# Half-array fp32 products of a hybrid decoder's mixers, issued with the halves alternating

## The chip, the cores and the metric

The kernel runs on one core of a Trainium2 chip. The metric is the device time of one execution in microseconds (us).

## What is computed

One inference step of a decoder trunk with two layers, for a prompt of 512 tokens and eight sample sequences of eight tokens each; all are held as 576 token columns. A layer normalizes the residual, projects it with one matrix, runs four token mixers on parts of the result, adds their output projection, and then an MLP:

```python
h = rmsnorm(x, P['norm_mix_w'][li])
proj = jnp.einsum('bld,de->ble', h, P['w_in'][li]).astype(jnp.float32)
...
mix = jnp.concatenate([y_ssd, y_swa, y_hg, y_lru], axis=-1).astype(dtype)
x = x + jnp.einsum('ble,ed->bld', mix, P['w_out'][li])
h2 = rmsnorm(x, P['norm_mlp_w'][li])
up = jnp.einsum('bld,df->blf', h2, P['w_up'][li])
x = x + jnp.einsum('blf,fd->bld', jnp.square(jax.nn.relu(up)), P['w_down'][li])
```

Three of the mixers have products of 64-wide heads: HGRN2 (a gated linear recurrence), SSD (Mamba-2) and attention in a sliding window. The two recurrences work in chunks. A chunk's output is the sum of a term from inside the chunk and one from the state before it, as here for HGRN2:

```python
o_intra = jnp.einsum('bchts,bcshv->bcthv', A, v)
...
o_inter = jnp.einsum('bcthk,bchkv->bcthv', q * jnp.exp(bc), S_in)
o = (o_intra + o_inter).reshape(b, nc * T, H, V)[:, :L]
```

## The kernel before, in words

Features lie on the partitions, tokens in the columns. The large products (`product`, line 336; the MLP's seven-product form at line 1089) split each fp32 operand into two parts that the array takes at one pass each and add three products per block; their results are called pi (input projection), pd (output and down projection), pu and p. The mixers' own products are plain fp32, and each of them appears in the profile as two instructions.

A recording layer takes the program in the order of the code and a scheduler orders each engine's instructions from it; each engine then runs its own queue in order. The projections of the next mixer fill PE's queue between the steps of the mixer before it.

The products that the change touches have two heads, or two groups, one on partitions 0 to 63 and the other on 64 to 127, and use 64 rows or 64 columns of the array, or both:

- HGRN2, `hgrn`, once for each of two pairs of heads per layer. After the four products u (line 578), from which VectorE (DVE) makes the running states hst (line 585), o is written by products of 128 rows and 64 columns (line 595, the term inside a chunk; four chunks, two heads) and added to by products of 64 rows and 64 columns (line 597, the term from the state, chunks 1 to 3). For every chunk and head the adding product follows the writing one. Then the samples' os, one head after the other: one writing product (line 603) and eight adding ones of eight columns (line 605). The products us (line 612) follow. DVE reads o at line 598 and os at line 606.
- SSD, `ssd`, for each of two groups g per layer: four products G (line 718; 64 rows, 128 columns) at the head of the group's turn and one Gs for the samples, later y (lines 781 and 783) and ys (lines 788 and 791), built as o and os are, with both halves j of the output on the same 64 rows in the adding products. DVE reads y at line 784 and ys at line 792.
- Attention, `swa`: the samples' aos (lines 941 and 943), then four blocks of queries in staggered steps: the logits lg (line 962), one kv head i after the other, and the output ao (line 993), head by head, each over its blocks of keys.

```python
for i in range(2):
    r = slice(64 * i, 64 * i + 64)
    for e in range(2):
        for k in range(nk):
```

PSUM tiles of the mixers come from `bank`: five banks in turn; the large products have three of their own.

Of the kernel before, what the change touches and what calls it, by code (L numbers as in the profile page):

```python
# [14 lines left out]
ALU = mybir.AluOpType  # L15
AX = mybir.AxisListType
PSUM = bass.MemoryType.PSUM
# [13 lines left out]
CW = 600                 # columns of a causal convolution over the padded row  # L31
# [15 lines left out]
# columns of the packed per-layer vectors  # L47
# [9 lines left out]
# columns of the constants  # L57
# [7 lines left out]
# tiles of 128 columns of w_in, in the order of their use  # L65
# [48 lines left out]
class Pool:  # L114
    """A pool of tiles by role: t(tag) allocates the next tile of that role."""
# [15 lines left out]
def seqs(t, w=NT):  # L131
    """the sample columns as [rows, sequence, w]; w = 11 in padded rows"""
    o = NP_ if w == NT else NP_ + 3
    return t[:, o : o + NB * w].rearrange("p (b t) -> p b t", b=NB)


def staggered(parts):
    """run the parts' steps so that each part is one step behind the one before it"""
    n = 0
    while parts:  # L140
        n += 1
        for p in parts[:n]:
            if next(p, True):
                parts.remove(p)
                n -= 1


class Kern:
# [14 lines left out]
    # ---- small helpers  # L163
# [28 lines left out]
    # ---- constants and everything that is loaded once  # L192
# [75 lines left out]
            # sample rows (r, e, t) of 32-row groups: sequence b = 4 * u + r, head 2 * i + e  # L268
# [11 lines left out]
    def lower_bounds(self):  # L280
        """log of HGRN's lower bound of layer 1 and of its complement (layer 0's bound is zero by construction)."""
# [25 lines left out]
    # ---- weights: float32 = hi + lo, both exact in float32r; eight blocks of 128 x 128  # L307
# [18 lines left out]
    def product(self, name, blocks, put):  # L326
        """put(half, columns, sum over the blocks (wh, wl, xh, xl) of w.T @ x in that half of the columns);
        behind a norm the first products run ahead of 1/rms, which their put() needs"""
# [17 lines left out]

    def silu(self, out, in_):
        return self.nc.scalar.activation(out, in_, AF.Silu)

    def exp_ln(self, ins):  # L350
        """the tables of exp and ln again, behind the last use of others"""
# [3 lines left out]
    # ---- RMSNorm over the model dimension: split (x * w) for the products, 1/rms as a factor of their results  # L355
# [31 lines left out]
    def rstd(self, r, sqs, scale, ones):  # L387
        """r = (mean over features + eps)^-1/2, on every partition; ones adds the rows that belong together."""
# [8 lines left out]
    # ---- input projection of one tile of columns -> [128, T] in PSUM, times 1/rms into dst  # L397
# [38 lines left out]
    def history(self, xp, hist, out):  # L436
        """the padded row's history columns, and the last three columns of each sequence as the new history"""
# [14 lines left out]
    def to_tokens(self, src, dst):  # L452
        """[128 features, T] -> tokens on partitions, [128, 4 x 128 | 128], the last block with 64 rows"""
# [10 lines left out]
    def by_sequence(self, dst, src):  # L464
        """dst [64, b, n] = src [64 tokens, n] in the rows of sequence b, else 0"""
# [19 lines left out]
    def hgrn(self, p):  # L485
# [6 lines left out]
        # log sigmoid(f), log f, k  # L492
# [29 lines left out]
        # pairs (s, t) by the level at which their blocks meet; every exponent is <= 0  # L522
# [37 lines left out]
        # c is now the running sum within a chunk  # L560
# [11 lines left out]
        # states  # L572
# [16 lines left out]
        # o  # L589
        ps = self.bank("o")  # L590
        for ci in range(4):
            a = slice(128 * ci, 128 * ci + 128)
            for d in range(2):
                r = slice(64 * d, 64 * d + 64)
                nc.tensor.matmul(ps[r, a], vt[:, 128 * ci + 64 * d : 128 * ci + 64 * d + 64], A[:, d, a], start=True, stop=ci == 0)  # L595
                if ci:
                    nc.tensor.matmul(ps[r, a], sts[ci][r], q[r, a], start=False, stop=True)
        V.tensor_tensor(o[:, :NP_], ps, o[:, :NP_], op=ALU.add)
        # samples
        p2 = self.bank("os")  # L600
        for d in range(2):
            r = slice(64 * d, 64 * d + 64)
            nc.tensor.matmul(p2[r, :NS], vt[:, NP_ + 64 * d : NP_ + 64 * d + 64], A[:, d, NP_:T], start=True, stop=False)
            for b in range(NB):
                nc.tensor.matmul(p2[r, NT * b : NT * b + NT], S0[r, b], q[r, NP_ + NT * b : NP_ + NT * b + NT], start=False, stop=b == NB - 1)  # L605
# [10 lines left out]
        # the norm by head, the gate  # L616
# [8 lines left out]
    # ---- SSD  # L625
# [3 lines left out]
    def ssd_dt(self):  # L629
        """dt, the running sum of dt * A, and exp(last - sum): rows = heads"""  # L630
# [27 lines left out]
        # tokens on partitions: [128, chunk, (dt | sum | exp(last - sum)), head]  # L658
# [9 lines left out]
        # C's factor exp(sum) for the two heads of a group, and its last values  # L668
# [12 lines left out]
    def ssd(self):  # L681
# [28 lines left out]
        sqs = []  # L710
        for g in range(2):
            rg = slice(64 * g, 64 * g + 64)
            # decay[s, t] = exp(sum_t - sum_s) where t >= s, times B_s . C_t
            gm = P.t("b", SLOT, bufs=2)
            ps = self.bank("G")
            for ci in range(4):
                a = slice(128 * ci, 128 * ci + 128)
                nc.tensor.matmul(ps[:, a], B[rg, a], C[rg, a], start=True, stop=True)
# [12 lines left out]
            # exp(min(., 0))  # L731
# [5 lines left out]
            # tokens on partitions: x dt, x dt exp(last - sum)  # L737
# [16 lines left out]
            # the states before each chunk and after the last one  # L754
# [19 lines left out]
            # y  # L774
            y, dp = X[g], self.par("sD", g)
            ps = self.bank("y")
            for j in range(2):
                r = slice(64 * j, 64 * j + 64)
                for ci in range(4):
                    a = slice(128 * ci, 128 * ci + 128)  # L780
                    nc.tensor.matmul(ps[r, a], xs[:, 128 * ci + 64 * j : 128 * ci + 64 * j + 64], D[j][:, a], start=True, stop=ci == 0)  # L781
                    if ci:
                        nc.tensor.matmul(ps[r, a], new[ci - 1][rg, j], self.cs[j][rg, a], start=False, stop=True)
            V.scalar_tensor_tensor(y[:, :NP_], y[:, :NP_], dp, ps, op0=ALU.mult, op1=ALU.add)
            p2 = self.bank("ys")
            for j in range(2):
                r = slice(64 * j, 64 * j + 64)
                nc.tensor.matmul(p2[r, :NS], xs[:, NP_ + 64 * j : NP_ + 64 * j + 64], D[j][:, NP_:T], start=True, stop=False)
                for b in range(NB):
                    a = slice(NP_ + NT * b, NP_ + NT * b + NT)  # L790
                    nc.tensor.matmul(p2[r, NT * b : NT * b + NT], S0T[rg, b, j], self.cs[j][rg, a], start=False, stop=b == NB - 1)  # L791
# [15 lines left out]
    # ---- RG-LRU  # L807
    def lru(self, xps, gs):
# [4 lines left out]
        # -8 softplus(-lambda)  # L813
# [12 lines left out]
        for p, xp in enumerate(xps):  # L826
# [8 lines left out]
            V.tensor_scalar(r[:, p, :CW], r[:, p, :CW], lr[:, p : p + 1], None, op0=ALU.mult)      # log a  # L835
        # gelu's tanh
# [13 lines left out]
        # 1 - a^2 = tanh(-log a) (1 + a^2)  # L850
# [6 lines left out]
        # the column before a sample's first token carries its state  # L857
# [15 lines left out]
    # ---- sliding-window attention; q tile e holds heads (e, 2 + e) on the partitions of kv heads (0, 1)  # L873
    def swa(self, Q, K, Vv):
# [23 lines left out]
        # samples: rows (r, e, t) in groups of 32, blocks (i, u), sequence b = 4 * u + r  # L898
# [7 lines left out]
        Ls = [P.t("L", [2, 256], bufs=4) for _ in range(2)]      # by kv head  # L906
# [31 lines left out]
        p2 = self.bank("aos")                            # [128 (i d), u, r, 32]  # L938
        for i in range(2):
            r = slice(64 * i, 64 * i + 64)  # L940
            nc.tensor.matmul(p2[r, :256], vts[:, r], pn[:64, i], start=True, stop=False)
            for b in range(NB):
# [438 lines left out]
```

## Time and profile before

| | |
|---|---|
| median of three runs | 1412.06 us (1411.49 to 1412.78) |
| span of the profiled execution | 1412.2 us |
| time of the profiled execution beside its span | none is given apart from the span; the median of the runs is 0.1 us under it |
| PE (matmul) busy | 1388.7 us, 98% |
| DVE busy | 1031.7 us, 73% |
| ACT busy | 651.7 us, 46% |
| first layer: mixers and output projection | 0 to 322 us |
| second layer: the same | 705 to 1013 us |

The rest of the span is the MLPs, 383 and 399 us. PE's records overlap, since matmuls are pipelined: the distance from a group's start to the next group's start tells what it costs, the duration of a record does not. The clock column (PEclk) is the share of TensorE's full clock that was granted in a stretch.

### The profile page before, as it was taken

The page shows a single profiled execution, that of the slowest core. Times are in us where ns is not written, and L with a number is a line of the kernel's source. Part 1 is how long each engine was busy: PE and PEld are TensorE (multiplying, and loading weights), DVE is VectorE, ACT ScalarE, POOL GpSimd, SP SyncE. Part 2 cuts the span into 40 slices and gives each one's busy share as a digit, 9 for nine tenths or more (in the row PEclk, how much of TensorE's full clock was granted, in tenths as well). Part 3 has the DMA queues.
Part 4 walks back from the last instruction along what each step waited for, and adds up shares of the span by engine and source line. Part 5 has one row for each costly group of instructions (what it writes and reads, how often), then busy time and mean ns, then how long its engine had stood idle before and what let it go on. Part 6 is the DMA issues. An engine that isn't in the chain of part 4 may idle for free.

```text
span 1412.2 us, 25457 instructions
## 1 busy us (share of the span) xinstructions
PE 1388.7 (98%) x10376; PEld 1326.4 (94%) x10376; DVE 1031.7 (73%) x2059; ACT 651.7 (46%) x1167; POOL 64.6 (5%) x125
## 2 busy tenths in 40 slices
PE   7999999999999999999999999999999999999997
PEld 7898889899999999999998989898999999999997
DVE  7966687668777778777668768764886877778765
ACT  6455427566433344333453734456662433343334
POOL 4010101100000000000000000010000000000000
PEclk9999999999999999999999999999999999999999
DMA  7142323312232223232330323130232223223221
GB/s 252 47 145 101 103 72 103 99 58 89 79 103 93 88 76 105 75 104 85 125 128 27 118 77 107 66 136 31 83 113 75 76 91 105 80 72 105 90 75 67
DMA packets 39716, 131.33 MB, mean 93 GB/s; under 512 B 5960, under 2 KB 8128, under 8 KB 39568
## 3 DMA queue, kind: packets, MB, share of 16 engines
q1 hardware_dynamic: 29312, 102.12, 21.2%
q0 software_dynamic: 6544, 22.65, 4.7%
q10 hardware_dynamic: 3744, 4.95, 1.0%
q8 instruction: 81, 1.33, 0.4%
q14 instruction: 35, 0.29, 0.1%
HBM read 120.32 MB, written 11.34 MB: 93 GB/s over the span
## 4 chain that ended last, share of the span: by engine, by line
PE 90%; DVE 4%; ACT 3%; issue 1%; DMA 1%; DVEq 0%; ACTq 0%
PE pd L336 33%; PE p L1089 21%; PE pi L336 16%; PE pu L336 5%; PE sc L544 2%; PE pl L1241 2%; PE ss L393 1%; PE ao L993 1%; PE y L781 1%; PE pdt L336 1%; PE o L595 1%; DMA cs<-acd 1%; PE os L605 1%; ACT hi L323 1%; PE ys L791 1%
## 5 line engine op out<-in xcount | busy, mean ns | idle before, releaser
L336 PE MATMUL pd<-fh,hi 128*128 128x288 f32 x960 | 283.8, 296 | 0.0
L336 PE MATMUL pd<-fl,hi 128*128 128x288 f32 x960 | 283.7, 296 | 0.0
L336 PE MATMUL pd<-fh,lo 128*128 128x288 f32 x960 | 283.6, 295 | 0.0
L323 ACT CAST hi<-raw 128x1024 fp32r<-128x1024 f32 x134 | 140.3, 1047 | 287.2 <-PE pd L336 154.6
L336 PE MATMUL pi<-xh,hi 128*128 128x288 f32 x704 | 213.4, 304 | 7.4 <-ACT xh L368 7.4
L336 PE MATMUL pi<-xl,hi 128*128 128x288 f32 x704 | 214.0, 304 | 0.7 <-DVE xl L369 0.7
L336 PE MATMUL pi<-xh,lo 128*128 128x288 f32 x704 | 213.9, 304 | 0.0
L323 DVE TENSOR_TENSOR lo<-raw,hi 128x1024 fp32r<-128x1024 f32 x134 | 163.6, 1221 | 24.3 <-ACT hi L323 23.4
L336 PEld LDWEIGHTS pd<-fh,hi 128*128 128x128 f32 x960 | 181.1, 189 | 0.0
L336 PEld LDWEIGHTS pd<-fl,hi 128*128 128x128 f32 x960 | 181.0, 189 | 0.0
L336 PEld LDWEIGHTS pd<-fh,lo 128*128 128x128 f32 x960 | 180.6, 188 | 0.0
L1024 DVE TENSOR_TENSOR x<-x,pd 128x288 f32<-128x288 f32 x240 | 107.9, 450 | 99.5 <-PE pd L336 99.3
L336 PEld LDWEIGHTS pi<-xh,hi 128*128 128x128 f32 x704 | 136.1, 194 | 11.7 <-ACT xh L368 7.4
L336 PEld LDWEIGHTS pi<-xh,lo 128*128 128x128 f32 x704 | 136.2, 193 | 4.2 <-issue 3.2
L336 PEld LDWEIGHTS pi<-xl,hi 128*128 128x128 f32 x704 | 135.9, 193 | 2.9 <-DVE xl L369 1.2
L1089 PE MATMUL p<-Th,ul 128*128 128x288 f32 x312 | 92.0, 295 | 0.0
L1089 PE MATMUL p<-Th,uh 128*128 128x288 f32 x312 | 92.0, 295 | 0.0
L1089 PE MATMUL p<-Tl,uh 128*128 128x288 f32 x312 | 92.0, 295 | 0.0
L1089 PE MATMUL p<-xh,ul 128*128 128x288 f32 x312 | 91.9, 295 | 0.0
L1089 PE MATMUL p<-xl,uh 128*128 128x288 f32 x312 | 91.7, 294 | 0.0
L1089 PE MATMUL p<-xh,uh 128*128 128x288 f32 x312 | 91.7, 294 | 0.0
L1065 ACT CAST uh<-raw 128x1024 fp32r<-128x1024 f32 x52 | 54.5, 1048 | 66.8 <-PE p L1089 44.1
(487 smaller groups left out, 3114.1 us busy)
## 6 DMA issues: line engine op xcount, KB each, us to landing
raw<-in_wu SPq DMA_DIRECT2D x64, 512.0 KB, 3.2
raw<-in_wd SPq DMA_DIRECT2D x64, 512.0 KB, 4.3
raw<-in_wi SPq DMA_DIRECT2D x44, 512.0 KB, 3.3
raw<-in_wo SPq DMA_DIRECT2D x16, 512.0 KB, 3.2
x<-in_xT SPq DMA_DIRECT2D x8, 288.0 KB, 5.5
a<-acd ACTq DMA_DIRECT2D x4, 576.0 KB, 3.9
xl<-in_xT POOLq DMA_DIRECT2D x8, 288.0 KB, 4.2
xd<-x POOLq DMA_DIRECT2D x8, 288.0 KB, 2.4
```

The lines of the kernel that those rows point to most:

```text
L323: self.split_ins = nc.scalar.copy(hi, raw).ins, nc.vector.tensor_tensor(lo, raw, hi.bitcast(F32), op=ALU.subtract).ins
L336: self.nc.tensor.matmul(out, w, x[:, a], start=n == 0, stop=n == last)
L393: nc.tensor.matmul(ps[:, :TH], ones, s[:, TH * h : TH * h + TH], start=n == 0, stop=n == len(sqs) - 1)
L544: nc.tensor.matmul(pv[:, :, 64 * ci : 64 * ci + 64], kE[:, 128 * ci : 128 * ci + 128], qE[:, :, 64 * ci : 64 * ci + 64], start=True, stop= ...
L595: nc.tensor.matmul(ps[r, a], vt[:, 128 * ci + 64 * d : 128 * ci + 64 * d + 64], A[:, d, a], start=True, stop=ci == 0)
L605: nc.tensor.matmul(p2[r, NT * b : NT * b + NT], S0[r, b], q[r, NP_ + NT * b : NP_ + NT * b + NT], start=False, stop=b == NB - 1)
L781: nc.tensor.matmul(ps[r, a], xs[:, 128 * ci + 64 * j : 128 * ci + 64 * j + 64], D[j][:, a], start=True, stop=ci == 0)
L791: nc.tensor.matmul(p2[r, NT * b : NT * b + NT], S0T[rg, b, j], self.cs[j][rg, a], start=False, stop=b == NB - 1)
L1024: self.nc.vector.tensor_tensor(y[:, a], x[:, a], ps, op=ALU.add)
L1065: S.copy(hl[0], src)
L1089: nc.tensor.matmul(ps[:, :TH], u, x, start=j == 0, stop=j == 11)
L1241: nc.tensor.matmul(ps, u[:, o + q], v[:, a], start=j == 0, stop=j == 11)
```

## The change

A helper `tiled` issues a list of products; o and os, y and ys, aos and ao are now lists in which all writing products come first and the adding ones behind them, with the two halves of the partitions taking turns in both. Only the first two products of a list are marked as starting an accumulation and only the last two as ending it. In SSD the G products of both groups are issued together ahead of the groups, alternating, into two banks. In attention both lg tiles of a block are made ahead, and their products alternate between the kv heads. Comments go too. The instructions of every engine are the same ones before and after; only their order differs.

```diff
+    def tiled(self, products):
+        for n, (out, w, x) in enumerate(products):
+            self.nc.tensor.matmul(out, w, x, start=n < 2, stop=n >= len(products) - 2, skip_group_check=True)
...
         ps = self.bank("o")
-        for ci in range(4):
-            a = slice(128 * ci, 128 * ci + 128)
-            for d in range(2):
-                r = slice(64 * d, 64 * d + 64)
-                nc.tensor.matmul(ps[r, a], vt[:, 128 * ci + 64 * d : 128 * ci + 64 * d + 64], A[:, d, a], start=True, stop=ci == 0)
-                if ci:
-                    nc.tensor.matmul(ps[r, a], sts[ci][r], q[r, a], start=False, stop=True)
+        self.tiled([(ps[64 * d : 64 * d + 64, 128 * ci : 128 * ci + 128], vt[:, 128 * ci + 64 * d : 128 * ci + 64 * d + 64],
+                     A[:, d, 128 * ci : 128 * ci + 128]) for ci in range(4) for d in range(2)]
+                   + [(ps[64 * d : 64 * d + 64, 128 * ci : 128 * ci + 128], sts[ci][64 * d : 64 * d + 64],
+                       q[64 * d : 64 * d + 64, 128 * ci : 128 * ci + 128]) for ci in range(1, 4) for d in range(2)])
...
+        self.tiled([(p2[half(d), :NS], vt[:, NP_ + 64 * d : NP_ + 64 * d + 64], A[:, d, NP_:T]) for d in range(2)]
+                   + [(p2[half(d), NT * b : NT * b + NT], S0[half(d), b], q[half(d), NP_ + NT * b : NP_ + NT * b + NT])
+                      for b in range(NB) for d in range(2)])
...
+        G = [self.bank("G") for g in range(2)]
+        for ci in range(4):
+            a = slice(128 * ci, 128 * ci + 128)
+            for g in range(2):
+                nc.tensor.matmul(G[g][:, a], B[64 * g : 64 * g + 64, a], C[64 * g : 64 * g + 64, a], start=True, stop=True)
         for g in range(2):
...
-            ps = self.bank("G")
-            for ci in range(4):
-                a = slice(128 * ci, 128 * ci + 128)
-                nc.tensor.matmul(ps[:, a], B[rg, a], C[rg, a], start=True, stop=True)
+            ps = G[g]
...
+            lg = [self.bank("lg").rearrange("p (e n) -> p e n", e=2) for i in range(2)]
+            for e in range(2):
+                for i in range(2):
+                    nc.tensor.matmul(lg[i][:, e, :n], Q[e][kv(i), a], K[kv(i), s0 : s0 + n], start=True, stop=True)
...
-            for i in range(2):
-                r = slice(64 * i, 64 * i + 64)
-                for e in range(2):
-                    for k in range(nk):
-                        kb = s0 // 128 + k
-                        nc.tensor.matmul(po[r, e], vt[:, 128 * kb + 64 * i : 128 * kb + 64 * i + 64],
-                                         PT[i][:, e, 128 * k : 128 * k + 128], start=k == 0, stop=k == nk - 1)
+            at = lambda i, k: s0 + 128 * k + 64 * i
+            self.tiled([(po[kv(i), e], vt[:, at(i, k) : at(i, k) + 64], PT[i][:, e, 128 * k : 128 * k + 128])
+                        for k in range(nk) for e in range(2) for i in range(2)])
```

The lists of y and ys and of aos are made in the same way.

Where the instructions stand. On PE, in the first HGRN2 pair of layer 0, behind the products u, the later part of o and os stood so before (a row is one program instruction, two in the profile; xN counts equal ones in a row; the numbers tell tiles apart):

```order
L595 MATMUL o_623<-A_157,vt_448 64x128
L597 MATMUL o_623<-q_307,hst_609 64x128
L595 MATMUL o_623<-A_157,vt_448 64x128
L597 MATMUL o_623<-q_307,hst_609 64x128
L595 MATMUL o_623<-A_157,vt_448 64x128
L597 MATMUL o_623<-q_307,hst_614 64x128
L595 MATMUL o_623<-A_157,vt_448 64x128
L597 MATMUL o_623<-q_307,hst_614 64x128
L603 MATMUL os_639<-A_157,vt_448 64x64
L605 MATMUL os_639<-q_307,S_54_437 64x8 x8
L603 MATMUL os_639<-A_157,vt_448 64x64
L605 MATMUL os_639<-q_307,S_54_437 64x8 x8
```

Now, all of o and os:

```order
L351 MATMUL o_623<-A_157,vt_448 64x128 x8
L351 MATMUL o_623<-q_307,hst_604 64x128 x2
L351 MATMUL o_623<-q_307,hst_609 64x128 x2
L351 MATMUL o_623<-q_307,hst_614 64x128 x2
L351 MATMUL os_639<-A_157,vt_448 64x64 x2
L351 MATMUL os_639<-q_307,S_54_437 64x8 x16
L614 MATMUL us_659<-t_660,f_165 64x512
L614 MATMUL us_659<-t_663,f_165 64x512
```

The writing products of o now stand together, the adding ones behind them by state, and both halves of os in one run; y and ys have the same pattern.

On PE, in the second HGRN2 pair of layer 1, the order now is mixed, with the projection products pi among them:

```order
L351 MATMUL o_9655<-A_7922,vt_9480 64x128 x8
L351 MATMUL o_9655<-q_9345,hst_9636 64x128
L336 MATMUL pi_9905<-xh_7879,hi_9901 128x288
L336 MATMUL pi_9905<-xl_7880,hi_9901 128x288
L351 MATMUL o_9655<-q_9345,hst_9636 64x128
L351 MATMUL os_9671<-A_7922,vt_9480 64x64
L351 MATMUL o_9655<-q_9345,hst_9641 64x128
L351 MATMUL os_9671<-A_7922,vt_9480 64x64
L351 MATMUL o_9655<-q_9345,hst_9641 64x128
L351 MATMUL os_9671<-q_9345,S_1314_9463 64x8 x11
L351 MATMUL o_9655<-q_9345,hst_9646 64x128
```

Here adding products of o have come apart and stand between writing and adding products of os; before, o and os followed each other as in the first pair, with five pi products between two of o's.

On PE, in the attention of layer 0, second block of queries, before:

```order
L993 MATMUL ao_2776<-PT_2758,vt_2555 64x128 x4
L993 MATMUL ao_2776<-PT_2759,vt_2555 64x128 x4
L962 MATMUL lg_2801<-x_2365,x_2424 128x256
L962 MATMUL lg_2801<-x_2365,x_2483 128x256
L962 MATMUL lg_2806<-x_2365,x_2424 128x256
L962 MATMUL lg_2806<-x_2365,x_2483 128x256
```

and now:

```order
L351 MATMUL ao_2776<-PT_2758,vt_2555 64x128
L959 MATMUL lg_2801<-x_2365,x_2424 128x256
L351 MATMUL ao_2776<-PT_2759,vt_2555 64x128
L351 MATMUL ao_2776<-PT_2758,vt_2555 64x128
L351 MATMUL ao_2776<-PT_2759,vt_2555 64x128
L351 MATMUL ao_2776<-PT_2758,vt_2555 64x128
L351 MATMUL ao_2776<-PT_2759,vt_2555 64x128
L351 MATMUL ao_2776<-PT_2758,vt_2555 64x128
L351 MATMUL ao_2776<-PT_2759,vt_2555 64x128
L959 MATMUL lg_2802<-x_2365,x_2424 128x256
```

The first ao product has come apart from the other seven, with a product lg of the next block between them.

## Rows read from the trace of the kernel before

**Rows 1.** Page of the profile, part 1, busy us

```profile
PE 1388.7 (98%) x10376; PEld 1326.4 (94%) x10376; DVE 1031.7 (73%) x2059; ACT 651.7 (46%) x1167; POOL 64.6 (5%) x125
```

**Rows 2.** Page, part 4, chain that ended last

```profile
PE 90%; DVE 4%; ACT 3%; issue 1%; DMA 1%; DVEq 0%; ACTq 0%
```

**Rows 3.** Timeline of PE, second HGRN2 pair, layer 0: start us, duration

```profile
203.88 0.65 PE L595 MATMUL o<-A,vt 128*64 128x128 f32 x6
204.46 0.43 PE L597 MATMUL o<-q,hst 64*64 64x128 f32 x2
204.82 0.43 PE L595 MATMUL o<-A,vt 128*64 128x128 f32 x2
...
208.43 0.33 PE L603 MATMUL os<-A,vt 128*64 128x64 f32 x2
208.68 1.09 PE L605 MATMUL os<-q,S 64*64 64x8 f32 x16
209.71 0.33 PE L603 MATMUL os<-A,vt 128*64 128x64 f32 x2
...
210.69 0.65 PE L612 MATMUL us<-t,f 64*64 64x512 f32 x2
...
211.70 0.41 PE L336 MATMUL pi<-xh,hi 128*128 128x288 f32 x1
```

**Rows 4.** Timeline of PE, attention, first query block, layer 0

```profile
274.48 0.65 PE L993 MATMUL ao<-PT,vt 128*64 128x128 f32 x4
275.06 0.70 PE L962 MATMUL lg<-x,x 64*128 64x256 f32 x2
```

**Rows 5.** Timeline of PE, SSD, first group, layer 0

```profile
128.13 0.65 PE L781 MATMUL y<-a,c 128*64 128x128 f32 x4
...
132.89 0.33 PE L788 MATMUL ys<-a,c 128*64 128x64 f32 x2
...
135.46 1.16 PE L718 MATMUL G<-X 64*128 64x128 f32 x8
```

**Rows 6.** Timeline of PE, the samples' attention, layer 0

```profile
264.45 0.64 PE L941 MATMUL aos<-PT,vt 64*64 64x256 f32 x2
...
267.67 1.68 PE L962 MATMUL lg<-x,x 64*128 64x128 f32 x16
```

**Rows 7.** Waits of DVE: us in total, times, longest

```profile
DVE X L784 <- PE y L783: 11.3, 4, 3.1
...
DVE o L598 <- PE o L597: 9.6, 4, 2.9
```

**Rows 8.** Windows, first mixer stage: busy us of each engine

```profile
0.00:322.00 322.00, 309.17 (x2279) 278.66 (x2280) 233.14 (x529) 169.59 (x324) 39.50 (x75) 0.97 0.32 109
```

**Rows 9.** Windows, the half-clock stretches of PE: first, sum of eight

```profile
72.08:78.90 6.82, 6.82 (x40) 0.50 0.05 17
...
sum 37.51, PE 37.51; mean PE 4.69
```

**Rows 10.** Timeline of PE up to 66.70 us, start of o, first HGRN2 pair

```profile
66.69 0.33 PE L595 MATMUL o<-A,vt 128*64 128x128 f32 x2
```

**Rows 11.** Groups of PE, 267.66 to 269.2 us: busy us, mean ns, idle us

```profile
L962 PE MATMUL lg<-x,x 64*128 64x128 f32 x8 | 0.7, 297 | 0.0
```

**Rows 12.** Windows of the ls products alone, layer 0: PE busy (count), clock

```profile
247.20:248.70 1.50, 1.41 (x64) 1.00 0.91 357
```

**Rows 13.** Chain of waits: start us, us

```profile
296.54 1.51 PE ao L993 x16
298.05 23.25 PE pd L336 x173
```

**Rows 14.** Timeline of PE, projection products inside a half-clock stretch

```profile
139.06 0.44 PE L336 MATMUL pi<-xh,hi 128*128 128x288 f32 x1
139.30 0.44 PE L336 MATMUL pi<-xl,hi 128*128 128x288 f32 x1
```

**Rows 15.** Timeline of DVE, states of the second HGRN2 pair, layer 0

```profile
203.82 1.84 DVE L585 SCALAR_TENSOR_TENSOR hst<-hst,c,u 64x64 f32<-64x64 f32 x6
```

More of the change, by code (lines that the diff above doesn't have):

```diff
@@ L590, in hgrn @@
         ps = self.bank("o")
-        for ci in range(4):
-            a = slice(128 * ci, 128 * ci + 128)
-            for d in range(2):
-                r = slice(64 * d, 64 * d + 64)
-                nc.tensor.matmul(ps[r, a], vt[:, 128 * ci + 64 * d : 128 * ci + 64 * d + 64], A[:, d, a], start=True, stop=ci == 0)
-                if ci:
-                    nc.tensor.matmul(ps[r, a], sts[ci][r], q[r, a], start=False, stop=True)
+        self.tiled([(ps[64 * d : 64 * d + 64, 128 * ci : 128 * ci + 128], vt[:, 128 * ci + 64 * d : 128 * ci + 64 * d + 64],
+                     A[:, d, 128 * ci : 128 * ci + 128]) for ci in range(4) for d in range(2)]
+                   + [(ps[64 * d : 64 * d + 64, 128 * ci : 128 * ci + 128], sts[ci][64 * d : 64 * d + 64],
+                       q[64 * d : 64 * d + 64, 128 * ci : 128 * ci + 128]) for ci in range(1, 4) for d in range(2)])
         V.tensor_tensor(o[:, :NP_], ps, o[:, :NP_], op=ALU.add)
         p2 = self.bank("os")
[L601 to L605, printed above, removed]
+        half = lambda d: slice(64 * d, 64 * d + 64)
+        self.tiled([(p2[half(d), :NS], vt[:, NP_ + 64 * d : NP_ + 64 * d + 64], A[:, d, NP_:T]) for d in range(2)]
+                   + [(p2[half(d), NT * b : NT * b + NT], S0[half(d), b], q[half(d), NP_ + NT * b : NP_ + NT * b + NT])
+                      for b in range(NB) for d in range(2)])
         V.tensor_tensor(o[:, NP_:T], p2[:, :NS], o[:, NP_:T], op=ALU.add)
@@ L776, in ssd @@
             ps = self.bank("y")
[L777 to L783, printed above, removed]
+            half, chunk = (lambda j: slice(64 * j, 64 * j + 64)), (lambda ci: slice(128 * ci, 128 * ci + 128))
+            self.tiled([(ps[half(j), chunk(ci)], xs[:, 128 * ci + 64 * j : 128 * ci + 64 * j + 64], D[j][:, chunk(ci)])
+                        for ci in range(4) for j in range(2)]
+                       + [(ps[half(j), chunk(ci)], new[ci - 1][rg, j], self.cs[j][rg, chunk(ci)])
+                          for ci in range(1, 4) for j in range(2)])
             V.scalar_tensor_tensor(y[:, :NP_], y[:, :NP_], dp, ps, op0=ALU.mult, op1=ALU.add)
             p2 = self.bank("ys")
[L786 to L791, printed above, removed]
+            self.tiled([(p2[half(j), :NS], xs[:, NP_ + 64 * j : NP_ + 64 * j + 64], D[j][:, NP_:T]) for j in range(2)]
+                       + [(p2[half(j), NT * b : NT * b + NT], S0T[rg, b, j], self.cs[j][rg, NP_ + NT * b : NP_ + NT * b + NT])
+                          for b in range(NB) for j in range(2)])
             V.scalar_tensor_tensor(y[:, NP_:T], y[:, NP_:T], dp, p2[:, :NS], op0=ALU.mult, op1=ALU.add)
@@ L938, in swa @@
         p2 = self.bank("aos")
-        for i in range(2):
-            r = slice(64 * i, 64 * i + 64)
-            nc.tensor.matmul(p2[r, :256], vts[:, r], pn[:64, i], start=True, stop=False)
-            for b in range(NB):
-                nc.tensor.matmul(p2[r, 32 * b : 32 * b + 16], vc[:, b, r], pc[:, i, 32 * b : 32 * b + 16], start=False, stop=b == NB - 1)
+        kv = lambda i: slice(64 * i, 64 * i + 64)
+        self.tiled([(p2[kv(i), :256], vts[:, kv(i)], pn[:64, i]) for i in range(2)]
+                   + [(p2[kv(i), 32 * b : 32 * b + 16], vc[:, b, kv(i)], pc[:, i, 32 * b : 32 * b + 16])
+                      for b in range(NB) for i in range(2)])
         pv = p2[:, :256].rearrange("p (b x t) -> p b x t", b=NB, x=4)
@@ L957, in block @@
             mx, sm, ng = (self.small([128, 4], c) for c in ("mx", "sm", "ng"))
+            lg = [self.bank("lg").rearrange("p (e n) -> p e n", e=2) for i in range(2)]
+            for e in range(2):
+                for i in range(2):
+                    nc.tensor.matmul(lg[i][:, e, :n], Q[e][kv(i), a], K[kv(i), s0 : s0 + n], start=True, stop=True)
             for i in range(2):
-                r = slice(64 * i, 64 * i + 64)
-                ps = self.bank("lg").rearrange("p (e n) -> p e n", e=2)
-                for e in range(2):
-                    nc.tensor.matmul(ps[:, e, :n], Q[e][r, a], K[r, s0 : s0 + n], start=True, stop=True)
                 for e in range(2):
                     h = 2 * i + e
-                    V.tensor_tensor_reduce(out=L[i][:, e, :n], in0=ps[:, e, :n], in1=bias[:, h, 256 - n :], scale=1.0,
+                    V.tensor_tensor_reduce(out=L[i][:, e, :n], in0=lg[i][:, e, :n], in1=bias[:, h, 256 - n :], scale=1.0,
                                            scalar=sinks[:, h : h + 1], op0=ALU.add, op1=ALU.max, accum_out=mx[:, h : h + 1])
@@ L987, in block @@
             po = self.bank("ao").rearrange("p (e n) -> p e n", e=2)[:, :, :128]
-            for i in range(2):
-                r = slice(64 * i, 64 * i + 64)
-                for e in range(2):
-                    for k in range(nk):
-                        kb = s0 // 128 + k
-                        nc.tensor.matmul(po[r, e], vt[:, 128 * kb + 64 * i : 128 * kb + 64 * i + 64],
-                                         PT[i][:, e, 128 * k : 128 * k + 128], start=k == 0, stop=k == nk - 1)
+            at = lambda i, k: s0 + 128 * k + 64 * i
+            self.tiled([(po[kv(i), e], vt[:, at(i, k) : at(i, k) + 64], PT[i][:, e, 128 * k : 128 * k + 128])
+                        for k in range(nk) for e in range(2) for i in range(2)])
             S.copy(oh[:, :, a], po)
```

## The prediction

> **What bounds the kernel now.** I read the busy times first: PE is busy in 98% of the 1412.2 us span [rows 1], and the chain that ended last lies on PE for 90%, DVE for 4%, ACT for 3% [rows 2]. The shown runs have their median at 1412.06 us, 0.1 below the profiled span; the sum is made against the span. A busy PE is no full PE, since records overlap, so the timeline comes next, where a group's cost is the distance from its start to the next group's. Each fp32 product is recorded as two instructions.
>
> In the timeline of the second HGRN2 pair of layer 0 [rows 3] the reader is to see three things. First, o costs 4.55 us (203.88 to 208.43) for 28 instructions, since writing products (128 rows by 64 columns) and adding ones (64 by 64) take turns: two instructions need 0.36 us. Four instructions of one form, all on one half, need 0.58 us [rows 4]. With a step s and a change of form c, 2s + c = 0.36 and 4s + c = 0.58, so s = 0.11 and c = 0.14 us. Second, os needs 1.03 us for 16 tiny adding instructions, and does that twice, one half after the other. Third, from the first o to the first projection product behind us it is 7.82 us. SSD's y and ys take 7.33 us, and G for one group 1.16 us [rows 5]; the samples' attention product aos takes 3.22 us [rows 6]. So these bursts are PE time in which half the array or less works.
>
> The same stretch of waits on DVE: 9.6 us for o and 11.3 us for y, four waits each [rows 7]. DVE idles through the bursts and is busy for only 233 of the first 322 us [rows 8]; shortening a burst moves both PE's queue and DVE's work forward.
>
> The TensorE clock is granted at half (1.2 instead of 2.4 GHz) in eight stretches, 37.5 us together [rows 9]. All eight begin inside or just behind such a burst, the first in os.
>
> **What the change does and costs.** No instruction is added or removed; the order of instructions on PE changes, and the scheduler moves some filling products with it. No DMA moves, and SP's queue is the same row for row.
>
> Do halves overlap? The first two o instructions of the first pair belong to the two column halves, and both had started by 66.70 us [rows 10]. Eight lg instructions (64 rows, 128 columns), whose halves of the rows are near enough in the queue to run together, are busy for 0.7 us [rows 11], against 1.16 us for eight G instructions of the same form on one half [rows 5]. The 64 ls instructions of 32 columns, four column places beside each other, go through in 1.41 us [rows 12], 22 ns each, so issuing is no limit at 58 to 64 ns for a pair. I therefore take one step s for a pair of instructions.
>
> - **o**: 16 writing instructions, 8 steps and a change: 8 x 0.11 + 0.14 = 1.02. Twelve adding, 6 x 0.11 + 0.14 = 0.80. Sum 1.82 instead of 4.55.
> - **os**: two writing pairs 0.25, then 16 adding pairs in the 1.03 that 16 instructions take now: 1.28. The products us behind them no longer slip in beside os; I give them all of 210.69 to 211.70, 1.01 [rows 3]. The block: 1.82 + 1.28 + 1.01 = 4.11 instead of 7.82, a gain of 3.71, four times 14.8. In the last of the four the scheduler still mixes forms; some five more changes and four pairs that don't meet take back 5 x 0.14 + 4 x 0.11 = 1.1, so 13.7.
> - **y and ys**: 1.82 + 1.28 = 3.10 instead of 7.33; 4.23 four times, 16.9.
> - **G**: both groups at once in eight steps, so one 1.16 us group per layer goes: 2.3.
> - **aos**: the two halves, 3.22 us one after the other, become one run of pairs, a gain of 1.6 per layer [rows 6]: 3.2.
> - **ao and lg** of the prompt: a block's 16 ao instructions take 1.51 us [rows 13], since the second half already catches up with the first in the queue, and could fall to 1.02; but in five of six such blocks the first ao product now stands apart from the rest, which costs a change or two. Between nothing and 6 x 0.49 = 2.9 I take 1.5, since the split eats most of a pair's gain.
>
> Sum at full clock: 13.7 + 16.9 + 2.3 + 3.2 + 1.5 = 37.6 us.
>
> *Clock.* At half clock a projection product takes 0.24 us [rows 14], at full 23.25 / 173 = 0.134 [rows 13], so a half-clock us does 0.56 us of work: the eight stretches cost 0.44 x 37.5 = 16.5 us. The bursts shrink to about half and are denser. Bounds: nothing is given back, or all 16.5; I take two thirds, 11, because the sparse part, os and ys, shrinks most.
>
> *New waits.* The adding products of o need the running states hst. Six state steps take 1.84 us from 203.82 [rows 15], two per chunk, so the second ends at 204.43 and the fourth at 205.05. PE would reach the adding pairs of chunks 2 and 3, which need them, at 203.88 + 1.02 + 0.22 = 205.12 and at 205.34. The cover is 0.3 us, thin. Behind a late state stand os, us and the next projections, in PE's order. The later filling products have other places too. Between 0 and 8 us (a DVE-paced stretch eating a us in each of eight blocks) I take 3.
>
> Forecast: 1412.2 - 37.6 - 11 + 3 = 1366.6, about **1367 us**.
>
> Two rules are weighed against this. The trace has, at the start of o, two column halves over all 128 rows started together [rows 10]. The Trainium skill, "TensorE: Matmul & The Clock Gate", Part 3, The mechanism, says that weight loads overlap running products only when the row groups differ; the rows speak against it, and by it the time would be that of the third rival below. For the two row halves that write one PSUM bank in o and os there is no row: lg's halves have a bank each. "TensorEngine Tiling (Array Packing)", Restrictions and Gotchas, Gotcha 1, of the Trainium skill says that different row tiles can't use one bank at the same time; no trace shows it yet, and by it the time would be that of the first rival.
>
> **The rivals.**
> 1. *The two row halves of o and os take turns at their common bank.* Twelve adding steps instead of six (+0.66) and 32 tiny ones instead of 16 (+1.03) per block: 1.69 x 4 = 6.8 less gain. The sparse stretch stays long, so I give it a third of the clock, 5.5: 1412.2 - 30.8 - 5.5 + 3 = 1379. For it: every overlapping row pair in the trace has two banks. Against: the halves also have separate output partitions. Chance 0.15.
> 2. *The PE time is saved, but the mixers are paced by DVE and ACT.* DVE is busy 233 of 322 us in the first mixer stage [rows 8], and its waits for ACT are not touched. If half of the 48.6 comes through: 1412.2 - 24.3 = 1388. Against: DVE waits for o and y itself [rows 7]. Chance 0.1.
> 3. *Column halves with the same rows don't overlap.* Only changes of form go, and the row-halved parts pair: o 16 x 0.11 + 0.14 + 0.80 = 2.70, os 4 x 0.11 + 1.03 = 1.47, so a block 5.18 (gain 2.64, four times 10.6 less 1.1); y 28 x 0.11 + 2 x 0.14 = 3.36 and ys 4 x 0.11 + 2 x 1.03 = 2.50 (gain 1.47, four times 5.9); G 2.3: 17.7, and 5.5 of clock: 1412.2 - 17.7 - 5.5 + 3 = 1392. Against: [rows 10]. Chance 0.05.
> 4. *Slower: each step to the other half drains the array like a change of form.* Place: the 30 steps per o-os or y-ys block where 14 changes stand now, 14 more in each aos, 15 in each G: 8 x 16 + 28 + 30 = 186 more, at 0.14 us 26 us: 1438. It decides as soon as an alternation costs more than a step and the pairs don't overlap. Against it stand [rows 10], where the other half's instruction started with no gap. Chance 0.03.
>
> That the change doesn't do what it says is excluded by the order of the built program for o, os, y, ys, aos and G; only the prompt's attention and the last HGRN2 pair keep mixed forms, which the sum has.
>
> **How the numbers follow.** The forecast has 0.66, the rivals 0.15, 0.1, 0.05 and 0.03, and 0.01 is left for effects that cancel. The likeliest case gives 1367. Its own range: all the clock back, no new wait and 2.9 for ao give 1412.2 - 39.0 - 16.5 = 1357; none of the clock back gives 1378. Rival 1, with no clock back, ends at 1384. The range is 1355 to 1385; outside lie rivals 2 to 4. A measurement of this kernel can tell 0.2%, 2.8 us, from no change. Faster by more than that are the forecast and rivals 1 to 3, 0.96; same 0.01; slower 0.03.
>
> **What would show it.** In the changed profile o should take about 1.8 us from its first start to os, os some 1.3 us, y and ys 3.1 together, one 16-instruction G per layer about as long as one of eight now, aos 1.6. Two o adding instructions should start within a few ns of each other; if they stand 0.11 us apart, rival 1 holds, and if y's writing pairs do so too, rival 3. DVE's waits for o and y should fall by more than half. The half-clock stretches should come down from eight to two or three. The forecast is wrong if PE stands idle behind o for hst, if DVE's busy share in the mixers doesn't rise, or if half-clock stretches turn up in other places, as between the attention's blocks.

## The result, and the profile after

The changed kernel takes 1361.76 us (median of four runs, 1358.82 to 1364.10), the kernel before on the same chip 1412.42 us (1411.49 to 1413.83): a ratio of 0.964, interval 0.962 to 0.966, or 50.7 us less. The forecast was 1367 us. The profiled execution took 1359.7 us with a span of 1357.2 us, 55.0 us below the span of before.

Part 1 of its page, busy times, and part 4, the chain that ended last, answer to [rows 1] and [rows 2]:

```profile
PE 1334.6 (98%) x10376; PEld 1287.3 (95%) x10376; DVE 1031.6 (76%) x2059; ACT 651.4 (48%) x1167; POOL 63.7 (5%) x125
...
PE 92%; DVE 4%; ACT 3%; issue 1%; DMA 0%; DVEq 0%; ACTq 0%
```

The work is the same, PE has 54 us less of it and is still the bound. The timeline of PE for the second HGRN2 pair of layer 0 answers to [rows 3]; columns are start and duration in us:

```profile
183.19 1.09 PE L351 MATMUL o<-A,vt 128*64 128x128 f32 x16
184.21 0.87 PE L351 MATMUL o<-q,hst 64*64 64x128 f32 x12
185.01 0.34 PE L351 MATMUL os<-A,vt 128*64 128x64 f32 x4
185.28 1.04 PE L351 MATMUL os<-q,S 64*64 64x8 f32 x29
186.12 0.64 PE L614 MATMUL us<-t,f 64*64 64x512 f32 x1
...
187.21 0.40 PE L336 MATMUL pi<-xh,lo 128*128 128x288 f32 x1
```

From start to start, o takes 1.82 us (4.55 before), os 1.11, us 1.09, and the whole block, from o to the first projection product, 4.02 instead of 7.82. SSD and G, for [rows 5], and the samples' attention, for [rows 6], in the same view:

```profile
121.72 1.09 PE L351 MATMUL y<-a,c 128*64 128x128 f32 x16
122.75 0.87 PE L351 MATMUL y<-cs,sst 64*64 64x128 f32 x12
123.55 0.34 PE L351 MATMUL ys<-a,c 128*64 128x64 f32 x4
...
124.85 0.55 PE L746 MATMUL xt<-cst,X 128*128 128x128 f32 x3
...
102.43 1.16 PE L717 MATMUL G<-X 64*128 64x128 f32 x16
103.52 0.33 PE L726 MATMUL Gs<-X 64*64 64x64 f32 x2
...
238.45 0.65 PE L351 MATMUL aos<-PT,vt 64*64 64x256 f32 x4
239.03 1.11 PE L351 MATMUL aos<-PT,vc 128*64 128x16 f32 x32
240.07 1.58 PE L959 MATMUL lg<-x,x 64*128 64x128 f32 x16
```

y and ys take 3.13 us instead of 7.33, sixteen G instructions 1.09 us, aos 1.62 instead of 3.22.

The waits of DVE on o and y, 9.6 and 11.3 us before [rows 7], read now (us in total, times, longest; the line numbers have moved, and y's wait is not among them any more):

```profile
DVE X L791 <- PE ys L351: 1.3, 3, 0.5
...
DVE o L601 <- PE o L351: 1.6, 2, 1.4
```

The TensorE clock is granted in full over the whole span but its last microseconds, which are at half in the kernel before as well. Two windows that hold the mixers of the two layers answer to the eight stretches of [rows 9] (busy us of PE, PEld, DVE, ACT, POOL, then the granted clock, DMA share and GB/s; one stretch of 3.41 us would make the clock 0.99):

```profile
0.00:309.00 309.00, 297.14 (x2396) 274.14 (x2397) 246.27 (x552) 181.05 (x343) 38.57 (x75) 1.00 0.35 117
...
692.00:967.00 275.00, 272.50 (x2240) 250.27 (x2240) 220.72 (x475) 160.55 (x299) 16.36 (x34) 1.00 0.25 87
```

One wait has grown. In SSD PE stands before the transposes xt. The timeline of PE there, with the idle time and its releaser in brackets, and that of DVE:

```profile
105.07 0.29 PE L336 MATMUL pi<-xh,hi 128*128 128x288 f32 x1
106.90 0.63 PE L746 MATMUL xt<-cst,X 128*128 128x128 f32 x4 [1.54 <-DVE b L727]
```

```profile
102.72 0.45 DVE L420 TENSOR_TENSOR z<-pi,ssq 128x288 f32<-128x288 f32 x1
104.92 1.22 DVE L323 TENSOR_TENSOR lo<-raw,hi 128x1024 fp32r<-128x1024 f32 x1 [1.75 <-ACT hi L323]
106.07 0.68 DVE L723 TENSOR_TENSOR b<-G,cst 128x512 f32<-128x512 f32 x1
106.67 0.21 DVE L727 TENSOR_TENSOR b<-Gs,cst 64x64 f32<-64x64 f32 x1
```

The G products of both groups end at 103.52, but DVE's reads of G and Gs stand behind lo in its queue, and lo waits for ACT. xt waits for DVE's read of Gs, the releaser shown; with the second group's G now holding one of the five banks, xt seems to get the one of Gs (read from this releaser and the program, not tried by itself). In the kernel before, xt waited 0.7 us, for its operand X from ACT; now the waits of xt are 1.9 us together.

Where the 55.0 us came from, as sums over the execution of the distances from each group's first start to the next other product (us):

| group | before | after |
|---|---|---|
| o | 18.2 | 7.8 |
| os and us | 15.1 | 9.1 |
| y | 18.6 | 7.3 |
| ys | 10.9 | 5.1 |
| G | 5.3 | 2.2 |
| aos | 6.6 | 3.2 |
| ao and lg | 22.5 | 18.7 |

That is 43.8 us. Outside these groups the same sums give 11.2 more: 5.3 in the projections pi, 3.6 in the sums of the norms (ss), 1.4 in Gs and 0.9 in the rest. The waits of xt, which have grown by 1.2 us, are in these distances already, so all of the 55.0 is placed.

Part of the 43.8 is clock: 11.7 us of the eight stretches lie inside the groups of the table, and at the prediction's rate of 0.44 they cost 5.2 us there. The same groups at full clock bear this out: os and us of the first pair take 5.2 us before, those of the others 3.3; one G takes 2.0, the others 1.1; and lg of the first two blocks takes 1.6 in layer 0 [rows 6] and 3.0 in layer 1, here in the timeline of PE before:

```profile
953.13 3.09 PE L962 MATMUL lg<-x,x 64*128 64x128 f32 x16
956.16 0.40 PE L336 MATMUL pd<-mixh,hi 128*128 128x288 f32 x1
```

So 38.6 us of the 43.8 are products. The whole of the stretches costs 16.5 us by that rate; 38.6 + 16.5, less the 1.2 us of xt's waits, is 53.9 of the 55.0.

### The profile page after: what moved, and what is told of

Its sections match the earlier page's. It is cut to its first block, busy times and chain, and to the rows that moved or that the text cites. A ratio compares the mean times of both kernels' runs of the same rounds, so it can differ in the third digit from the quotient of the medians.

```text
span 1357.2 us, 25456 instructions
## 1 busy us (share of the span) xinstructions
PE 1334.6 (98%) x10376; PEld 1287.3 (95%) x10376; DVE 1031.6 (76%) x2059; ACT 651.4 (48%) x1167; POOL 63.7 (5%) x125
## 4 chain that ended last, share of the span: by engine, by line
PE 92%; DVE 4%; ACT 3%; issue 1%; DMA 0%; DVEq 0%; ACTq 0%
PE pd L336 34%; PE p L1083 21%; PE pi L336 18%; PE pu L336 6%; PE sc L550 2%; PE pl L1235 2%; PE ss L399 1%; PE pdt L336 1%; PE ao L351 1%; PE pt L983 1%; PE o L351 1%; ACT hi L323 1%; PE lg L959 1%; PE y L351 1%; DVE lo L323 0%
## 5 line engine op out<-in xcount | busy, mean ns | idle before, releaser
L336 PE MATMUL pi<-xh,hi 128*128 128x288 f32 x704 | 210.5, 300 | 7.4 <-ACT xh L374 7.4
L336 PE MATMUL pi<-xl,hi 128*128 128x288 f32 x704 | 211.1, 300 | 0.7 <-DVE xl L375 0.7
L336 PE MATMUL pi<-xh,lo 128*128 128x288 f32 x704 | 210.4, 299 | 0.0
L336 PEld LDWEIGHTS pi<-xh,hi 128*128 128x128 f32 x704 | 133.1, 190 | 11.1 <-ACT xh L374 7.4
L336 PEld LDWEIGHTS pi<-xh,lo 128*128 128x128 f32 x704 | 133.2, 189 | 3.9 <-issue 3.3
```

The costliest lines, as they stand in the source:

```text
L336: self.nc.tensor.matmul(out, w, x[:, a], start=n == 0, stop=n == last)
```

## Experiments

The first four ran on one chip, where the kernel before took 1414.34 us (nine runs), the other four on another, with 1413.93 us (sixteen runs). Sums as in the table above; the half-clock column leaves out the end of the span.

| kernel | median us | ratio (interval) | o | y | os, ys | G | half clock |
|---|---|---|---|---|---|---|---|
| changed, again | 1359.52 | 0.961 (0.959 to 0.963) | 7.8 | 7.3 | 10.7 | 2.2 | 6.8 |
| grouped, halves in sequence | 1380.34 | 0.975 (0.974 to 0.977) | 10.6 | 10.3 | 16.4 | 2.2 | 13.6 |
| alternating, forms mixed | 1368.81 | 0.967 (0.965 to 0.969) | 10.1 | 9.7 | 10.0 | 2.2 | 0 |
| G as before | 1363.11 | 0.964 (0.962 to 0.966) | 7.8 | 7.5 | 10.8 | 4.3 | 6.8 |
| HGRN2 alone | 1390.76 | 0.984 (0.982 to 0.986) | 7.8 | 18.6 | 16.6 | 5.3 | 13.7 |
| SSD alone | 1393.07 | 0.985 (0.983 to 0.987) | 18.2 | 7.3 | 16.8 | 2.2 | 20.5 |
| attention alone | 1408.59 | 0.996 (0.994 to 0.997) | 18.2 | 18.6 | 22.1 | 6.2 | 47.8 |
| late half first | 1354.66 | 0.958 (0.956 to 0.960) | 7.3 | 7.3 | 10.0 | 2.2 | 3.4 |

**The changed kernel again**, with no edit.

> The changed kernel again, for its spread. Its four runs came at 1358.8 to 1364.1 us, two near 1359 and two near 1364. Theory (bursts shorter by 37.6 us, half-clock stretches gone): 1359 to 1364, o 1.83 us, y 1.83 us, and no half-clock stretch or one of 3.4 us. Rival (the clock is only partly back, and the profiled execution was a lucky one): two or more half-clock stretches in the mixers and 1364 us or more.

It took 1359.52 us (1358.74 to 1363.77); its profiled execution was the longest of these, with a span of 1361.7 us. The timeline of PE shows why: PE reaches xt at the same place but waits longer, and a half-clock stretch begins before the wait is over.

```profile
104.80 0.29 PE L336 MATMUL pi<-xh,hi 128*128 128x288 f32 x1
108.91 1.09 PE L746 MATMUL xt<-cst,X 128*128 128x128 f32 x4 [3.82 <-DVE b L727]
```

```profile
107.84:114.67 6.83, 5.76 (x25) 5.75 (x26) 3.72 (x9) 5.00 (x6) 0.00 (x0) 0.50 0.55 163
```

The wait is 2.3 us longer than in the first trace, and the 5.76 us in which PE is busy at half clock cost 2.5 by the prediction's rate; 4.8 together, where the spans differ by 4.5. So this one wait accounts for the difference between these two executions, and may well hold the spread between 1359 and 1364 us, though the others have no trace. What sets the length of the wait from one execution to the next was not tried. The theory allowed a stretch of half this length; the rival's two or more stretches and its 1364 us did not come.

**Grouped, but the halves one after another.** Writing products first, then the adding ones, and in each the whole of one half before the other.

```diff
-    def tiled(self, products):
+    def tiled(self, products, nw):
-        for n, (out, w, x) in enumerate(products):
+        L = len(products)
+        order = [*range(0, nw, 2), *range(1, nw, 2), *range(nw, L, 2), *range(nw + 1, L, 2)]
...
+        for n in order:
+            out, w, x = products[n]
```

> The changed kernel, but in each list the halves come one after the other: all writing products of half 0, then of half 1, then the adding ones of half 0, then of half 1. Theory (a step of 0.11 us for a pair, 0.14 us for a change of form): only the overlap that the queue finds by itself is left, so o some 2.5 us instead of 1.83, os 2.1 instead of 1.3, aos 2.6 instead of 1.62: 12 us in eight blocks, 2 in aos, and some half-clock stretches come back (0 to 8 us): 1374 to 1385 us. Rival (the gain is from fewer changes of form, the halves' turns don't matter): as the changed kernel, 1362 us.

It took 1380.34 us. The same HGRN2 pair in the timeline of PE:

```profile
193.36 1.58 PE L355 MATMUL o<-A,vt 128*64 128x128 f32 x16
194.87 1.14 PE L355 MATMUL o<-q,hst 64*64 64x128 f32 x12
195.94 0.34 PE L355 MATMUL os<-A,vt 128*64 128x64 f32 x4
196.21 1.65 PE L355 MATMUL os<-q,S 64*64 64x8 f32 x29
197.66 0.65 PE L618 MATMUL us<-t,f 64*64 64x512 f32 x2
```

o takes 2.58 us, between the 4.55 of before and the 1.82 of the change; os 1.72 up to us, against 1.11. The time lies in the range that was expected, and the rival's 1362 us falls. This kernel, which groups by form and leaves G and lg alternating, is 34.0 us faster than the one before, with 3.1 of them in G; alternating the halves in the lists is worth another 20.8, in which 6.8 us less of half clock have their part. The 20.8 would be nothing if the halves could not run beside each other.

**Alternating, but with writing and adding pairs in turn** in o and y, chunk by chunk (ad holds the adding products).

```diff
+        wr = [(ps[64 * d : 64 * d + 64, 128 * ci : 128 * ci + 128], vt[:, 128 * ci + 64 * d : 128 * ci + 64 * d + 64],
+               A[:, d, 128 * ci : 128 * ci + 128]) for ci in range(4) for d in range(2)]
...
+        self.tiled(wr[:2] + [x for k in range(3) for x in wr[2 * k + 2 : 2 * k + 4] + ad[2 * k : 2 * k + 2]])
```

> The changed kernel, but o and y go chunk by chunk: writing pair, adding pair, writing pair, and so on; os, ys, aos, ao, G and lg stay as changed. Theory: 14 steps of 0.11 and six changes of 0.14 us, 2.38 us for o and for y instead of 1.83, eight times: 4.4 us more, 1366 us. Rival (pairing does little, the form changes were all): o near 3.9 us, 17 us more, 1378 us.

It took 1368.81 us (1363.95 to 1370.96). The timeline of PE, o of the same pair:

```profile
184.76 0.66 PE L351 MATMUL o<-A,vt 128*64 128x128 f32 x8
185.35 0.44 PE L351 MATMUL o<-q,hst 64*64 64x128 f32 x4
185.72 0.44 PE L351 MATMUL o<-A,vt 128*64 128x128 f32 x4
186.08 0.44 PE L351 MATMUL o<-q,hst 64*64 64x128 f32 x4
186.45 0.44 PE L351 MATMUL o<-A,vt 128*64 128x128 f32 x4
186.82 0.44 PE L351 MATMUL o<-q,hst 64*64 64x128 f32 x4
187.19 0.34 PE L351 MATMUL os<-A,vt 128*64 128x64 f32 x4
```

Two pairs and a change of form take 0.36 to 0.37 us: twice s plus c, as the prediction read them from single products. o takes 2.42 us, 0.6 more than grouped, for four more changes of form, 0.15 each. That is 4.7 us over the eight bursts, as expected, and the rival's 3.9 us for o falls. The time rose by 9.3, though the profiled execution, one of the two short ones of five, has a span of 1361.3 us. What the longer runs add is not in a trace.

**G one group at a time, as before**, all else changed.

```diff
-        G = [self.bank("G") for g in range(2)]
...
-            ps = G[g]
+            ps = self.bank("G")
+            for ci in range(4):
+                a = slice(128 * ci, 128 * ci + 128)
+                nc.tensor.matmul(ps[:, a], B[rg, a], C[rg, a], start=True, stop=True)
```

> The changed kernel with SSD's G products as they were before, one group at a time in one bank. Theory (G in pairs saves 1.09 us per layer, but its two banks bring a wait of 1.5 us of the transposes xt in layer 0): both go, 0.7 us more or less, 1361 to 1363 us, and PE's wait for DVE ahead of xt is gone. Rival (that wait is cover and costs nothing): 2.2 us more, 1364 us.

It took 1363.11 us. xt is there released by ACT again, as in the kernel before, so the wait on DVE comes with making both G at once (timeline of PE):

```profile
102.28 1.16 PE L720 MATMUL G<-X 64*128 64x128 f32 x8
103.36 0.33 PE L724 MATMUL Gs<-X 64*64 64x64 f32 x2
...
104.04 0.66 PE L744 MATMUL xt<-cst,X 128*128 128x128 f32 x4 [0.35 <-ACT X L354]
```

G costs 2.2 us more, the wait is gone, and two half-clock stretches (3.41 us each, 1.5 us of cost each) begin just behind the second group's G, one in each layer, which neither theory nor rival had. Both G at once is the better choice in spite of its wait, by 3.6 us in the medians, though the single times overlap (1358.74 to 1363.77 and 1362.43 to 1368.74).

**The parts alone.** In each kernel one mixer's function is that of the change, the other two are those of before; as an example HGRN2 alone, against the kernel before:

```diff
         ps = self.bank("o")
-        for ci in range(4):
...
+        self.tiled([(ps[64 * d : 64 * d + 64, 128 * ci : 128 * ci + 128], vt[:, 128 * ci + 64 * d : 128 * ci + 64 * d + 64],
```

> The change in HGRN2 alone (o and os); SSD and attention as before. Theory: the parts are worth what their own products lose and the half-clock stretches behind them. o and os lose 13.7 us by the prediction's sum; the stretches at 72.08, 212.02, 771.81 and 898.1 us in the trace of before, of 6.83 and three times 3.41 us, cost half their length, 8.5 us, of which the products themselves hold a part: about 20 us, so 1392 us (1388 to 1396), o at 1.83 us in the trace, no half-clock stretch behind o, those behind y and ys still there. Rival: the clock comes back only when all bursts are short (the stretches move to SSD and attention); then 13.7 us, 1398 us, with seven or eight stretches left.

> The change in SSD alone (G, y and ys); HGRN2 and attention as before. Theory: y and ys lose 16.9 us and G 2.3 us by the prediction's sum, the stretches at 136.93, 154.0 and 829.84 us go (about 6 us beside the products), and the new wait of xt costs 1.8 us: about 24 us, so 1388 us (1384 to 1393), y at 1.83 us in the trace. Rival: the clock comes back only when all bursts are short; then 17 us, 1395 us. With the run of HGRN2 alone and that of attention alone the three gains add up to the whole change's 51 us by the theory, to some 36 us by the rival.

> The change in attention alone (aos, lg and ao); HGRN2 and SSD as before. Theory: aos loses 3.2 us, lg and ao 1.5 us, the stretch at 952.72 us goes (about 1.5 us): 6 us, so 1406 us (1404 to 1409). Rival: the logits and outputs stand behind DVE's and ACT's steps of the blocks, and nothing but aos counts: 1409 us.

Measured: HGRN2 alone 1390.76, SSD alone 1393.07, attention alone 1408.59 us; gains of 23.2, 20.9 and 5.3 us. They add up to 49.4, beside 50.7 and 54.8 for the whole change in its two sets of runs. The rival, a clock that comes back only when all bursts are short, asked for some 36, and falls. HGRN2 alone has three half-clock stretches, all of them in SSD or attention. SSD alone is just outside its range of 1384 to 1393 us and nearer to its rival's 1395 than to 1388; its profiled execution, at 1388.88 the shortest of five, is not the one that would show why. In that execution five stretches are left, 20.5 us together, as much as those of HGRN2 and attention in the kernel before; they only move a little. The two below lie in or behind os of HGRN2 in layer 0, 3.41 and 6.83 us long, where the kernel before has 6.83 and 3.41 (windows, columns as above, and the sum over all five):

```profile
75.61:79.02 3.41, 3.41 (x13) 2.37 (x11) 2.67 (x7) 0.77 (x2) 0.56 (x1) 0.50 0.21 79
195.08:201.91 6.83, 6.83 (x33) 4.82 (x32) 1.51 (x3) 1.72 (x4) 1.08 (x2) 0.50 0.15 46
...
sum 20.47, PE 20.47 PEld 14.68 DVE 10.54 ACT 6.15 POOL 3.46; mean PE 4.09 PEld 2.94 DVE 2.11 ACT 1.23 POOL 0.69
```

With attention alone the time does not tell its two theories apart, since its profiled execution has a stretch of 17 us at half clock in and behind HGRN2, which it leaves as it was. Its products do: ao falls from 12.4 to 9.8 us, besides aos, so the rival's "nothing but aos" is wrong. lg falls from 10.2 to 8.9 us, but the half-clock stretch at 952.72 us, which is gone, held 1.4 of it; at full clock lg gains nothing.

**The half that is ready last goes first**, in ao and in the adding products of o.

```diff
-                       q[64 * d : 64 * d + 64, 128 * ci : 128 * ci + 128]) for ci in range(1, 4) for d in range(2)])
+                       q[64 * d : 64 * d + 64, 128 * ci : 128 * ci + 128]) for ci in range(1, 4) for d in (1, 0)])
...
-                        for k in range(nk) for e in range(2) for i in range(2)])
+                        for k in range(nk) for e in range(2) for i in (1, 0)])
```

> The changed kernel with the half that becomes ready last issued first in each pair of ao and of the adding products of o, so that the scheduler puts nothing between the first product of ao and the rest. Theory: ao's sixteen instructions then run as one burst in all blocks, at about 1.05 us instead of 0.36 and 1.02 us for the two pieces; seven such blocks, 0.3 us each: ao's total in the trace 7.6 us instead of 9.8, and the time 1357.3 us (1356 to 1359). Rival: the first product ran in a gap in which PE had nothing to do, so that the total stays at 9.8 us with what PE waits for it counted, and the time at 1359.5 to 1360 us.

It took 1354.66 us (1353.66 to 1358.04), a ratio of 0.958 (0.956 to 0.960), below its range of 1356 to 1359 us and faster than both kernels. A block of the attention in the changed kernel, and in this one (timelines of PE):

```profile
253.26 0.43 PE L351 MATMUL ao<-PT,vt 128*64 128x128 f32 x2
253.62 0.70 PE L959 MATMUL lg<-x,x 64*128 64x256 f32 x2
254.25 1.09 PE L351 MATMUL ao<-PT,vt 128*64 128x128 f32 x14
255.26 1.13 PE L959 MATMUL lg<-x,x 64*128 64x256 f32 x6
```

```profile
255.32 1.09 PE L351 MATMUL ao<-PT,vt 128*64 128x128 f32 x16
256.35 1.14 PE L959 MATMUL lg<-x,x 64*128 64x256 f32 x8
257.41 0.40 PE L336 MATMUL pd<-mixh,lo 128*128 128x288 f32 x1
```

ao and lg, 3.06 us up to the next pd in the changed kernel, need 2.09. Over the execution ao falls from 9.8 to 7.3 us and lg, which was split by the same first product, from 8.9 to 7.3. That is 4.1 us; o, os and us give another 0.8, in the last HGRN2 pair, where forms were mixed. The medians differ by 4.9, on two chips. The expectation had left lg and that pair out.

## Why the prediction was right

**The products.** The two constants, s for a step and c for a change of form, carried over from single products to pairs: o was predicted at 1.82 us and takes that, the block of o, os and us at 4.11 and takes 4.02, y and ys at 3.10 and take 3.13, aos at 1.6 and takes 1.62. The sixteen tiny pairs take the time of sixteen single ones, as the prediction had it: in the timeline of PE the 32 adding instructions of ys in SSD's second group of layer 0, with nothing between them, take 1.03 us up to the next product, against 1.03 for sixteen of os before [rows 3].

```profile
136.99 1.10 PE L351 MATMUL ys<-cs,S0T 64*64 64x8 f32 x32
138.02 0.75 PE L399 MATMUL ss<-z,ones 128*128 128x288 f32 x2
```

In the block of o, three of them slip in beside us, and os takes 1.11 instead of 1.28. Sixteen instructions of both G take as long as eight of one, as the run with G as before shows beside it (1.08 from 102.28 to 103.36); the prediction took 1.16 for it, the duration of the record and not the distance.

At full clock the groups lost 14.4 us in HGRN2, 16.4 in y and ys, 2.2 in G, 3.2 in aos and 2.4 in ao and lg, where the prediction has 13.7, 16.9, 2.3, 3.2 and 1.5.

**The rivals.** The first, row halves that take turns at a common bank, falls. In the timeline of PE cut at 184.22 us, two adding instructions have started within 0.01 us. They are of the two halves, on different rows and in one bank, since the two of one product start 0.16 us apart (204.46 and 204.62 in the kernel before):

```profile
184.21 0.33 PE L351 MATMUL o<-q,hst 64*64 64x128 f32 x2
```

Twelve take 0.80 us, against 1.07 with the halves in sequence (194.87 to 195.94). By the rule of the Trainium skill, "TensorEngine Tiling (Array Packing)", Restrictions and Gotchas, Gotcha 1, this pair would not go; here the halves write separate output partitions of the bank, and the trace disagrees with the rule in this form. The third, column halves on the same rows that do not overlap, falls by y: sixteen writing instructions in 1.03 us, and twelve adding ones, both halves on the same 64 rows, in 0.80. There the trace disagrees as well with the rule on row groups in "TensorE: Matmul & The Clock Gate", Part 3, The mechanism, of the Trainium skill, as the third rival reads it. The second rival, DVE and ACT as the bound, falls by PE, which is busy for 98% of the span as before, and by DVE's waits for o, which went from 9.6 to 1.6 us; DVE's busy share in the first mixer stage rose from 72% (233 of 322 us) to 79% (232 of 292). The fourth, a drain at each alternation, would have lengthened every burst; none was.

**The terms that were off.** The clock: the prediction took 11 of 16.5 us back, and in the profiled execution all 16.5 came back. It expected two or three stretches and the first trace has none; in two other traces of kernels with both G at once (the changed kernel again, and the late half first) a stretch of 6.8 or 3.4 us is left about xt.

The new waits: 3 us were taken, mostly for the states hst. In layer 0's second pair DVE makes the six state steps from 183.13 in 1.84 us, 0.31 each, so the fourth ends at 184.36; PE starts the adding products at 184.21 and comes to the pair that needs that state after two others of two steps each, at 184.65. That is the cover of 0.3 us that the prediction had, and it held, so this wait cost nothing. The wait that did grow stands elsewhere: the part on G counted its products and not the bank that the second group's G holds while DVE is late. That was a mechanism missed, at 1.2 us in the first trace and at 3.5 and a half-clock stretch in the second; that the 3 us came near it is luck.

Attention's prompt blocks were taken at 1.5 us and gave 2.4 at full clock, all of it in ao; the split of ao, which the prediction set against a pair's gain, costs 4.1 us, which the last run got back.

Where the prediction had 37.6 us of products, 11 of clock and 3 of waits, the profiled execution has 38.6, 16.5 and 1.2, and 1.1 us that these three don't place: 9.4 us more gain. The medians, 1361.76 and 1359.52 us, lie 5.2 and 7.5 us under the forecast; the one slower execution with a trace has the longer wait of xt and the stretch beside it.

## What to carry to other kernels

Where a kernel has products that use half the array, read two prices from its timeline before anything else, that of a step and that of a change of form; here they predicted bursts of pairs to a tenth of a us. Grouping by form and alternating the halves are separate gains (some 31 and 21 us here), and the half whose operand comes last should lead each pair, or the scheduler fills the gap with other work and pays two changes of form. When products for two groups are made at once, count the PSUM banks that they hold until the slowest reader has come.

## What the hardware did that was not expected

The stretches of half clock were not only in the sparse bursts. With these shortened, one of 6.83 us came in a place where PE stood idle, 4.1 us without a start before xt, and in the last run one of 3.41 us behind 2.2 us without a start there. Idle time is not the only thing that comes before them: the two in the run with G as before begin behind G, where PE had not stood still.
